# A decoder layer on one core: a fourth quad of w_down row tiles by Strassen's scheme with its first sum made by transfers, splits queued behind two merges, and a later load of x

## The chip, the cores and the metric

The kernel runs on one NeuronCore of a Trainium2 chip. A core has TensorE (matmuls, results into PSUM), VectorE, ScalarE and GpSimd (elementwise work), SyncE (here it only issues transfers), and 16 DMA engines that all queues share. Each engine works through its own queue in order and waits on semaphores of the others. The metric is device microseconds of one execution, given as the median of several runs; the profile is of one further execution.

## The reference

One layer on a sequence of 256 tokens of width 1024, all in float32:

```python
proj = x @ w_in                                   # three attention mixers read its columns
o_a, o_b, o_c = dsa_mixer(...), dilated_mixer(...), moba_mixer(...)
gates = sigmoid(x @ w_gate).reshape(256, 3, 1024)
merged = gates[:, 0] * (o_a @ w_br_a) + gates[:, 1] * (o_b @ w_br_b) + gates[:, 2] * (o_c @ w_br_c)
x = layer_norm(ALPHA * x + merged @ w_out, ln1_g, ln1_b)
h = square(relu(x @ w_up)) @ w_down               # 1024 -> 4096 -> 1024
ple = sigmoid(x @ w_ple_gate) * (p @ w_ple)
x = layer_norm(ALPHA * x + h + ple, ln2_g, ln2_b)
```

## The kernel before, in words

**Precision.** Every float32 operand is split in two float32r parts, `hi` (a copy in the shorter format, by ScalarE, line 75) and `lo` (the rest, a subtraction by VectorE, line 79), and a product is three matmuls, hi-hi, hi-lo and lo-hi (`prod`, line 134). Each weight is brought in as 128 x 1024 pieces of 512 KB and split as it arrives.

**`Weights` (lines 50 to 90)** keeps the list of these pieces in the order of their use. `get(i)` returns the split piece i and writes the instructions of all pieces up to i + `AHEAD` (4): a load on SP's queue into one of five `raw` buffers, the ScalarE cast, the VectorE subtraction into one of five `whi` and `wlo` buffers (or into a place given). `after` is a tuple of instructions: what is written while it is set is put behind them on their own engines' queues (`issue_after`), which fixes an order and adds no wait across engines. A scheduler then orders each queue from the written program, its priorities and its buffers.

**The stages.** After attention, `merge(p)` (line 559, four of them) multiplies the first branch into PSUM, forms the gated sum on VectorE (lines 568 and 569), and makes two row blocks `mt` by a scaling on ScalarE (line 572) and a subtraction on VectorE (line 573). `outp` (a `Wide`, line 524) is `merged @ w_out`: eight row tiles of `w_out`, four by `step` and four by `finish`, the last four split straight into a part of `hA` (shown as `hT`). `PL` first holds x: line 596 loads it, 1 MB, from ScalarE's queue, and line 597 the rows of the first layer norm (`rows1`, 1 MB broadcast). `ln1` (line 621) reads both. Then follow the `w_ple` product, `w_ple_gate`, and `w_up`: 32 blocks of 128 features (loop at line 676), whose squares are split into `hT` (plain) or, for the first 4 x `QUADS` blocks, gathered in `four`, summed (line 710) and split as a quad.

**`w_down` (lines 723 to 830).** Its 32 row tiles of 128 are contracted in two ways. A *plain* row tile takes 2 token blocks x 2 column halves x 3 matmuls of 512 columns. Four row tiles with the two token blocks and two column halves are a 2 x 2 by 2 x 2 block product, a *quad*: Strassen's scheme in Winograd's form needs 7 products instead of 8, each of 2 x 3 matmuls of 512 columns. Sums on the activation side are those of line 710; on the weight side `quad(u)` makes t1 = b - a, t2 = c - t1, t3 = c - b and t4 = d - t2 on VectorE (line 742) from the blocks a, b, c, d that SP loads (line 736). `order` mixes three quad products with two plain rows; the last `LAST` (6) plain rows are kept for the end, where each output block is finished in turn and normalised by `ln2` (line 815). Eight PSUM banks collect the products P1, P5, P6, P7 and the output blocks 11, 12, 21, 22; lines 803 to 813 add them. `rows2`, the second norm's rows, takes the buffer of `four` (tag `rows`, one buffer) and is loaded at line 724, ahead of the stage.

The change touches lines 40, 556 to 582, 596 and 597, 708 to 724, 735 to 757 and 802 to 811.

Of the kernel before, what the change touches and what calls it, by code (L numbers as in the profile page):

```python
# [11 lines left out]
F32 = mybir.dt.float32  # L12
F32R = mybir.dt.float32r
ALU = mybir.AluOpType
# [5 lines left out]
D = 1024  # L20
# [16 lines left out]
    0, 384, 448, 512, 1024, 1088, 1096, 1864, 2120, 2376, 2760, 3144)  # L37

AHEAD = 4
QUADS = 3  # L40
LAST = 6
FIRST = 4
DV = 640
# [50 lines left out]
def hybrid_layer(ctx: ExitStack, tc: tile.TileContext, x0, xn, pT, wqk, wva, wvb, wg, wbc, wba,  # L94
                 wout, wup, wdq, wdn, wpg, wple, lnrow, rel, mask, out):
    nc = tc.nc
    pe, act, dve, pool = nc.tensor, nc.scalar, nc.vector, nc.gpsimd

    keep = ctx.enter_context(tc.tile_pool(name="keep", bufs=1))
    raw = ctx.enter_context(tc.tile_pool(name="raw", bufs=5))  # L100
# [349 lines left out]
    for j in range(2):  # L450
# [8 lines left out]
        o = opair()  # L459
# [93 lines left out]
                    done(b, c, self.acc[b][c])  # L553

    T2 = (slice(0, 128), slice(128, 256))
    mt = []


    def merge(p):
        hi, lo = W.get(u_ba[p][0])  # L560
        ps = mmbank(512).rearrange("p (f s) -> p f s", f=2)
        for f in range(2):
            for k in range(3):
                c = slice((3 * f + k) * 128, (3 * f + k + 1) * 128)
                prod(ps[:, f], (hi[:, c], lo[:, c]), (op[:, k, 0], op[:, k, 1]), k == 0, k == 2)
        g6 = G[:, 6 * p:6 * p + 6].rearrange("p (f i) s -> p f i s", f=2)
        g = g6[:, :, 0]
        dve.scalar_tensor_tensor(g, g, 1.0, ps, op0=ALU.add, op1=ALU.mult)
        dve.tensor_tensor(g, g, g6[:, :, 1], op=ALU.add)
        for f in range(2):  # L570
            m = qpool.tile([128, 2, S], F32R, name="q", tag="q")
            act.mul(m[:, 0], g[:, f], 0.5)
            dve.scalar_tensor_tensor(m[:, 1], g[:, f], 0.5, m[:, 0].bitcast(F32), op0=ALU.mult,
                                     op1=ALU.subtract)
            mt.append(m)

    outp = Wide(u_out, lambda k, b: (mt[k][:, 0, T2[b]], mt[k][:, 1, T2[b]]))
    for p in range(4):
        merge(p)
    for k in range(4):  # L580
        outp.step(k)
    mid.close()


# [7 lines left out]
    def row_load(t, i):  # L592
        act.dma_start(t, lnrow[i:i + 2].rearrange("r d -> (r d)").partition_broadcast(128)
                      .rearrange("p (r d) -> p r d", r=2))

    act.dma_start(PL, xn)
    row_load(rows1, 0)

    st = {}

# [75 lines left out]
    for f in range(32):  # L676
        ps = mmbank(512).rearrange("p (b a t) -> p b a t", b=2, a=2)
        hi, lo = W.get(u_up[f][0])
        cs = [slice(k * 128, (k + 1) * 128) for k in range(KT)]
        for k in range(KT):  # L680
            pe.matmul(ps, lhsT=hi[:, cs[k]], rhs=x1[:, :, k], start=k == 0, stop=False)  # L681
        for k in range(KT):
            pe.matmul(ps[:, :, 0], lhsT=lo[:, cs[k]], rhs=x1[:, :, k, 0], start=False,  # L683
                      stop=k == KT - 1)
        r = w2.tile([128, 2, 128], F32, name="r", tag="r")
        dve.tensor_reduce(r, ps.rearrange("p b a t -> p b t a"), axis=AX.X, op=ALU.add)  # L686
        act.activation(r, r, AF.Relu)
        u, m = divmod(f, 4)
        if u >= QUADS:
            q = w2.tile([128, S], F32, name="q2", tag="q2")  # L690
            act.activation(q, r.rearrange("p b t -> p (b t)"), AF.Square)
            h = hT[:, f - 4 * QUADS]
            act.copy(h[:, 0], q)
            dve.tensor_tensor(h[:, 1], q, h[:, 0].bitcast(F32), op=ALU.subtract)
            continue
        g = four[:, u % 2]
        act.activation(g[:, :, m], r, AF.Square)
        if m % 2 == 0:
            continue
        hi, lo, y = ((hQ[:, u, 0, 0], hQ[:, u, 0, 1], g[:, 0, 0:2]) if m == 1 else  # L700
                     (hQ[:, u, 1:3, 0], hQ[:, u, 1:3, 1], g[:, :, 2:4]))
        act.copy(hi, y)
        dve.tensor_tensor(lo, y, hi.bitcast(F32), op=ALU.subtract)
        if m == 1:
            continue
        a11, a21, a12, a22 = g[:, 0, 0:2], g[:, 1, 0:2], g[:, 0, 2:4], g[:, 1, 2:4]
        z = w2.tile([128, 4, 2, 128], F32, name="s", tag="s", bufs=1)
        for o, a, b, f2 in ((0, a21, a22, ALU.add), (2, a11, a21, ALU.subtract),
                            (1, z[:, 0], a11, ALU.subtract), (3, a12, z[:, 1], ALU.subtract)):
            dve.tensor_tensor(z[:, o], a, b, op=f2)  # L710
        if u < 2:
            parts = [(z, hS[:, u, 0], hS[:, u, 1])]
            sums.append([(hS[:, u, 0, i], hS[:, u, 1, i]) for i in range(4)])
        else:
            ts = [[qpool.tile([128, 2, S], F32R, name="q", tag="q")
                   .rearrange("p m (j t) -> p m j t", j=2) for _ in range(2)] for _ in range(2)]
            parts = [(z[:, 2 * i:2 * i + 2], *ts[i]) for i in range(2)]
            sums.append([(ts[i // 2][0][:, i % 2], ts[i // 2][1][:, i % 2]) for i in range(4)])
        for y, hi, lo in parts:
            act.copy(hi, y)  # L720
            dve.tensor_tensor(lo, y, hi.bitcast(F32), op=ALU.subtract)

    rows2 = p3.tile([128, 2, D], F32, name="rows", tag="rows")
    row_load(rows2, 2)


    xw = x1.rearrange("p b k a s -> p (b k a s)").rearrange("p (k a c) -> p k a c", k=2, a=2)

    def quad(u):

        t = {}

        def load(*names):
            for n in names:
                t[n] = raw.tile([128, 1024], F32, name="raw", tag="raw")
                nc.sync.dma_start(t[n], wdq[u, "abcd".index(n)])
            return t[names[0]]

        def less(n, x, y):
            p = p3 if n == "t1" else raw  # L740
            t[n] = p.tile([128, 1024], F32, name="raw", tag="raw")
            dve.tensor_tensor(t[n], t[x], t[y], op=ALU.subtract)  # L742
            return t[n]

        A = [(hQ[:, u, m, 0], hQ[:, u, m, 1]) for m in range(3)]
        Z = sums[u]
        return [(lambda: load("a", "b"), A[0], "P1"), (lambda: less("t1", "b", "a"), Z[0], "P5"),
                (lambda: load("c"), Z[3], "12"), (lambda: less("t3", "c", "b"), Z[2], "P7"),
                (lambda: less("t2", "c", "t1"), Z[1], "P6"), (lambda: load("d"), A[1], "11"),
                (lambda: less("t4", "d", "t2"), A[2], "21")]  # L750

    todo = [x for u in range(QUADS) for x in quad(u)]
    plain = list(range(NP))
    order = []
    while todo:
        order += todo[:3] + plain[:2]
        todo, plain = todo[3:], plain[2:]
    order += plain
    left = {"P1": 2 * QUADS, "P5": 2 * QUADS, "P6": 2 * QUADS, "P7": 2 * QUADS,
            "11": 2 * QUADS + NP, "12": 2 * QUADS + NP, "21": 2 * QUADS + NP, "22": NP - LAST}  # L760
# [38 lines left out]
    p1, p5, p6, p7 = (acc["P" + n] for n in "1567")  # L799
    u2, u3 = Y[:, 0, H[0]], Y[:, 0, H[1]]  # L800
    blk = [[PL[:, b, H[c]] for c in range(2)] for b in range(2)]
    tt = lambda o, a, b: dve.tensor_tensor(o, a, b, op=ALU.add)
    tt(blk[0][0], p1, blk[0][0])
    act.copy(u3, p1)
    tt(u2, p6, u3)
    tt(u3, p7, u2)
    tt(u2, p5, u2)
    tt(blk[0][1], u2, blk[0][1])
    tt(blk[1][0], u3, blk[1][0])
    tt(u3, p5, u3)  # L810
    tt(blk[1][1], u3, blk[1][1])
    end = [[acc["11"], acc["12"]], [acc["21"]] + [next(ps_a)[:, 0:256] for _ in range(2)]]
    tt(blk[1][1], acc["22"], blk[1][1])
# [116 lines left out]
```

## Time and profile before

| | us |
|---|---|
| median of 3 runs | 442.63 (442.06 to 443.55) |
| the profiled execution | 442.14 |
| its span | 440.4 |
| from the first merge's stretch to TensorE's start on `w_out` | 193.0 to 206.3 |
| `w_up` stage | 259.6 to 348.95 |
| `w_down` stage, to TensorE's last matmul | 348.95 to 432.2 |

Each group's row of the profile names the line, the engine, the operation, what is written and read, and the mean time of one instruction. The waits say which engine was idle ahead of which line and what ended the idle time. The chain of waits is followed back from the last instruction: at each step to what released it, or to the instruction before it on its engine. A matmul of 512 columns shows 0.39 us of its own, but the next starts 0.23 us later, since they are pipelined; the time from start to start is what counts.

### The profile page before, as it was taken

The page shows a single profiled execution, that of the slowest core. Times are in us where ns is not written, and L with a number is a line of the kernel's source. Part 1 is how long each engine was busy: PE and PEld are TensorE (multiplying, and loading weights), DVE is VectorE, ACT ScalarE, POOL GpSimd, SP SyncE. Part 2 cuts the span into 40 slices and gives each one's busy share as a digit, 9 for nine tenths or more (in the row PEclk, how much of TensorE's full clock was granted, in tenths as well). Part 3 has the DMA queues.
Part 4 walks back from the last instruction along what each step waited for, and adds up shares of the span by engine and source line. Part 5 has one row for each costly group of instructions (what it writes and reads, how often), then busy time and mean ns, then how long its engine had stood idle before and what let it go on. Part 6 is the DMA issues. An engine that isn't in the chain of part 4 may idle for free.

```text
span 440.4 us, 7719 instructions
## 1 busy us (share of the span) xinstructions
PE 429.0 (97%) x2837; PEld 388.7 (88%) x2837; DVE 337.4 (77%) x602; ACT 269.8 (61%) x487; POOL 101.7 (23%) x98
## 2 busy tenths in 40 slices
PE   8999999999999999998999999999999999999992
PEld 8999999999999999998886888888888888888882
DVE  4978977475664588768958779999888978588956
ACT  6775375584787766855605567888877765456500
POOL 3564355397543644400001000000000000000001
PEclk9999999999999999999999999999999999999998
DMA  8896765448544345467860866668655364655502
GB/s 282 316 313 219 238 187 176 158 129 314 161 148 130 124 152 164 140 193 288 258 265 0 281 221 185 187 193 284 198 183 183 105 212 144 250 151 204 226 0 96
DMA packets 27113, 84.29 MB, mean 191 GB/s; under 512 B 2820, under 2 KB 6828, under 8 KB 26692
## 3 DMA queue, kind: packets, MB, share of 16 engines
q1 hardware_dynamic: 25872, 79.54, 55.5%
q10 hardware_dynamic: 1140, 4.19, 2.6%
q8 instruction: 22, 0.36, 0.3%
q14 instruction: 15, 0.12, 0.1%
q0 software_dynamic: 64, 0.07, 0.1%
HBM read 81.90 MB, written 1.90 MB: 190 GB/s over the span
## 4 chain that ended last, share of the span: by engine, by line
PE 93%; DVE 2%; DMA 2%; issue 2%; ACT 1%; POOL 0%; POOLq 0%; DVEq 0%; ACTq 0%
PE mm L134 39%; PE b L134 23%; PE mm L681 13%; PE mm L683 7%; PE b L273 3%; PE b L407 3%; DMA raw<-in_wout_dram 2%; PE b L129 1%; PE b L319 1%; ACT whi L75 0%; PE b L320 0%; PE b L322 0%; PE b L321 0%; PE b L312 0%; PE b L314 0%
## 5 line engine op out<-in xcount | busy, mean ns | idle before, releaser
L79 DVE TENSOR_TENSOR wlo<-raw,whi 128x1024 fp32r<-128x1024 f32 (+5 forms) x147 | 157.4, 1085 | 42.1 <-ACT whi L75 38.6
L75 ACT CAST whi<-raw 128x1024 fp32r<-128x1024 f32 (+3 forms) x147 | 147.8, 1011 | 57.4 <-PE mm L134 17.2
L79 POOL TENSOR_TENSOR wlo<-raw,whi 128x384 fp32r<-128x384 f32 (+3 forms) x58 | 77.3, 1342 | 81.8 <-ACT whi L75 67.2
L134 PE MATMUL mm<-xl,whi 128*128 128x256 f32 x336 | 95.5, 284 | 0.0
L134 PE MATMUL mm<-xh,whi 128*128 128x256 f32 x336 | 95.1, 283 | 0.0
L134 PE MATMUL mm<-xh,wlo 128*128 128x256 f32 x336 | 95.0, 283 | 0.0
L134 PEld LDWEIGHTS mm<-xl,whi 128*128 128x128 f32 x336 | 63.3, 188 | 0.9
L681 PE MATMUL mm<-x,whi 128*128 128x512 f32 x256 | 64.1, 392 | 0.0
L134 PEld LDWEIGHTS mm<-xh,wlo 128*128 128x128 f32 x336 | 63.3, 188 | 0.6
L134 PEld LDWEIGHTS mm<-xh,whi 128*128 128x128 f32 x336 | 63.3, 188 | 0.2
L612 POOL TENSOR_TENSOR rs<-rs,half 128x1 f32<-128x1 f32 x4 | 4.1, 1028 | 246.0 <-DVE rs L611 246.0
L134 PE MATMUL b<-whi,hT 128*128 128x512 f32 (+1 forms) x176 | 55.0, 379 | 0.0
L681 PEld LDWEIGHTS mm<-x,whi 128*128 128x128 f32 x256 | 46.1, 189 | 8.3
L134 PEld LDWEIGHTS b<-whi,hT 128*128 128x128 f32 x176 | 32.7, 188 | 6.2
L683 PEld LDWEIGHTS mm<-x,wlo 128*128 128x128 f32 x256 | 34.9, 190 | 2.5
L683 PE MATMUL mm<-x,wlo 128*128 128x256 f32 x256 | 35.7, 282 | 0.0
L134 PE MATMUL b<-wlo,hT 128*128 128x512 f32 (+1 forms) x88 | 33.4, 380 | 0.0
L686 DVE TENSOR_REDUCE r<-mm 128x256 f32<-128x512 f32 x32 | 22.0, 687 | 5.9 <-PE mm L683 5.9
L134 PE MATMUL mm<-op,whi 128*128 128x256 f32 x128 | 23.3, 281 | 0.0
L742 DVE TENSOR_TENSOR raw<-raw 128x1024 f32<-128x1024 f32 x12 | 14.7, 1222 | 9.2 <-DMA raw<-in_wdq_dram 9.2
L134 PE MATMUL b<-whi,x 128*128 128x512 f32 x64 | 20.5, 396 | 0.3 <-ACT x L634 0.3
L240 ACT ACTIVATE G<-mm 128x256 f32<-128x256 f32 x24 | 9.2, 382 | 18.3 <-PE mm L134 18.2
(171 smaller groups left out, 712.2 us busy)
## 6 DMA issues: line engine op xcount, KB each, us to landing
raw<-in_wup_dram SPq DMA_DIRECT2D x32, 512.0 KB
raw<-in_wg_dram SPq DMA_DIRECT2D x24, 512.0 KB
raw<-in_wdn_dram SPq DMA_DIRECT2D x20, 512.0 KB
raw<-in_wqk_dram SPq DMA_DIRECT2D x18, 512.0 KB
raw<-in_wdq_dram SPq DMA_DIRECT2D x12, 512.0 KB
raw<-in_wout_dram SPq DMA_DIRECT2D x8, 512.0 KB
raw<-in_wpg_dram SPq DMA_DIRECT2D x8, 512.0 KB
T<-tabd SPq DMA_DIRECT2D x24, 128.0 KB
```

The source lines that it names most:

```text
L75: nc.scalar.copy(hi, r)
L79: e.tensor_tensor(lo[:, c], r[:, c], hi[:, c].bitcast(F32), op=ALU.subtract)
L129: pe.transpose(t[:, 0:128], ident, ident)
L134: pe.matmul(ps, lhsT=a[x], rhs=b[y], start=first and i == 0, stop=last and i == 2)
L240: act.activation(G[:, n_g[0]], ps, AF.Tanh, scale=0.5)
L273: m = pe.matmul(ss[h][:, QC[b]], lhsT=q[d, x, c], rhs=k[d, y, 0:128 * (b + 1)], start=i == 0, stop=i == 2)
L319: pe.matmul(v[:, 0:S], lhsT=V[:, 0, vh], rhs=hi[:, 256:512], start=True, stop=False)
L407: pe.matmul(first[f], lhsT=w[:, k, 128 * f:128 * f + 128], rhs=x[:, k], start=k == i == 0, stop=k == KT - 1 and i == 2)
L681: pe.matmul(ps, lhsT=hi[:, cs[k]], rhs=x1[:, :, k], start=k == 0, stop=False)
L683: pe.matmul(ps[:, :, 0], lhsT=lo[:, cs[k]], rhs=x1[:, :, k, 0], start=False, stop=k == KT - 1)
L686: dve.tensor_reduce(r, ps.rearrange("p b a t -> p b t a"), axis=AX.X, op=ALU.add)
L742: dve.tensor_tensor(t[n], t[x], t[y], op=ALU.subtract)
```

## The change

`QUADS` goes from 3 to 4, so sixteen row tiles of `w_down` are done in quads and sixteen plainly, and `order` takes one plain row for each three quad products. The quad's first sum t1 is now a + b: SP loads b into one half of `pair`, and a transfer that GpSimd issues adds a onto it; the signs of the other sums and of P5 change with it. `pair` takes the buffer of `four`; the first two quads' t1 are asked for behind the `w_up` stage, the third's and fourth's when t2 of the first and second is made. t2 = t1 + c goes into a buffer of its own, t3 = t2 - a into a's, t4 = t2 + d into d's, and P6 now comes ahead of P7. `rows2` is loaded behind the stage's splits. After each of the first two merges `W.after` is set to that merge's last scaling and subtraction, so that splits written later queue behind these on ScalarE and VectorE, until the fourth `step` of `outp` is written. The loads of x and of `rows1` queue on ScalarE behind the scalings of the third merge.

```diff
-QUADS = 3
+QUADS = 4
...
-    mt = []
+    mt, muls = [], []
...
         for f in range(2):
             m = qpool.tile([128, 2, S], F32R, name="q", tag="q")
-            act.mul(m[:, 0], g[:, f], 0.5)
-            dve.scalar_tensor_tensor(m[:, 1], g[:, f], 0.5, m[:, 0].bitcast(F32), op0=ALU.mult,
-                                     op1=ALU.subtract)
+            muls.append(act.mul(m[:, 0], g[:, f], 0.5).ins)
+            low = dve.scalar_tensor_tensor(m[:, 1], g[:, f], 0.5, m[:, 0].bitcast(F32),
+                                           op0=ALU.mult, op1=ALU.subtract)
             mt.append(m)
+        if p < 2:
+            W.after = (muls[-1], low.ins)
...
     for k in range(4):
         outp.step(k)
+    W.after = ()
     mid.close()
...
-    act.dma_start(PL, xn)
-    row_load(rows1, 0)
+    with tc.issue_after(muls[5]):
+        act.dma_start(PL, xn)
+        row_load(rows1, 0)
...
-        for o, a, b, f2 in ((0, a21, a22, ALU.add), (2, a11, a21, ALU.subtract),
-                            (1, z[:, 0], a11, ALU.subtract), (3, a12, z[:, 1], ALU.subtract)):
+        for o, a, b, f2 in ((0, a21, a22, ALU.subtract), (2, a11, a21, ALU.subtract),
+                            (1, z[:, 0], a11, ALU.subtract), (3, a12, z[:, 1], ALU.add)):
...
-    rows2 = p3.tile([128, 2, D], F32, name="rows", tag="rows")
-    row_load(rows2, 2)
-
+    pair = p3.tile([128, 2, D], F32, name="rows", tag="rows")
+
+    def first_sum(u):
+
+        if u < QUADS:
+            nc.sync.dma_start(pair[:, u % 2], wdq[u, 1])
+            pool.dma_start(pair[:, u % 2], wdq[u, 0], accum_op=ALU.add)
+
+    for u in range(2):
+        first_sum(u)
...
-        def load(*names):
-            for n in names:
-                t[n] = raw.tile([128, 1024], F32, name="raw", tag="raw")
-                nc.sync.dma_start(t[n], wdq[u, "abcd".index(n)])
-            return t[names[0]]
-
-        def less(n, x, y):
-            p = p3 if n == "t1" else raw
-            t[n] = p.tile([128, 1024], F32, name="raw", tag="raw")
-            dve.tensor_tensor(t[n], t[x], t[y], op=ALU.subtract)
+        def load(n):
+            t[n] = raw.tile([128, 1024], F32, name="raw", tag="raw")
+            nc.sync.dma_start(t[n], wdq[u, "abcd".index(n)])
+            return t[n]
+
+        def have():
+            t["t1"] = pair[:, u % 2]
+            return t["t1"]
+
+        def make(n, x, y, f):
+            t[n] = t[y]
+            if n == "t2":
+                t[n] = p3.tile([128, 1024], F32, name="raw", tag="raw")
+            dve.tensor_tensor(t[n], t[x], t[y], op=f)
+            if n == "t2":
+                first_sum(u + 2)
             return t[n]
...
-        return [(lambda: load("a", "b"), A[0], "P1"), (lambda: less("t1", "b", "a"), Z[0], "P5"),
-                (lambda: load("c"), Z[3], "12"), (lambda: less("t3", "c", "b"), Z[2], "P7"),
-                (lambda: less("t2", "c", "t1"), Z[1], "P6"), (lambda: load("d"), A[1], "11"),
-                (lambda: less("t4", "d", "t2"), A[2], "21")]
+        return [(lambda: load("a"), A[0], "P1"), (have, Z[0], "P5"),
+                (lambda: load("c"), Z[3], "12"),
+                (lambda: make("t2", "t1", "c", ALU.add), Z[1], "P6"),
+                (lambda: make("t3", "t2", "a", ALU.subtract), Z[2], "P7"),
+                (lambda: load("d"), A[1], "11"),
+                (lambda: make("t4", "t2", "d", ALU.add), A[2], "21")]
...
-        order += todo[:3] + plain[:2]
-        todo, plain = todo[3:], plain[2:]
+        order += todo[:3] + plain[:1]
+        todo, plain = todo[3:], plain[1:]
...
-    tt = lambda o, a, b: dve.tensor_tensor(o, a, b, op=ALU.add)
+    rows2 = p3.tile([128, 2, D], F32, name="rows", tag="rows")
+    row_load(rows2, 2)
+    tt = lambda o, a, b, f=ALU.add: dve.tensor_tensor(o, a, b, op=f)
...
-    tt(u2, p5, u2)
+    tt(u2, p5, u2, ALU.subtract)
...
-    tt(u3, p5, u3)
+    tt(u3, p5, u3, ALU.subtract)
```

## The prediction

> **What bounds the kernel now.** I read the page's busy shares, its 40 slices and its chain first, then the waits of TensorE, then stretches of the program.
>
> ```profile
> PE 429.0 (97%) x2837; PEld 388.7 (88%) x2837; DVE 337.4 (77%) x602; ACT 269.8 (61%) x487; POOL 101.7 (23%) x98
> ...
> PEclk9999999999999999999999999999999999999998
> ...
> PE 93%; DVE 2%; DMA 2%; issue 2%; ACT 1%; POOL 0%; POOLq 0%; DVEq 0%; ACTq 0%
> ```
>
> TensorE is busy 97% of the span at the full granted clock, and 93% of the chain that ended last is its work. So a change pays in two ways only: fewer matmuls, or less time in which TensorE waits. The waits of TensorE, then four stretches (length, PE, PEld, DVE, ACT, POOL, clock, DMA share, GB/s):
>
> ```profile
> PE b L129 <- POOL ident masks.py:199: 1.6, 1, 1.6
> PE b L134 <- ACT q L572: 1.1, 1, 1.1
> PE b L134 <- ACT x L634: 0.3, 1, 0.3
> ...
> 193.00:206.27 13.27, 12.16 (x106) 11.96 (x104) 9.98 (x15) 7.02 (x11) 0.00 (x0) 1.00 0.79 277
> 206.27:235.00 28.73, 28.71 (x128) 23.22 (x128) 23.93 (x37) 12.54 (x20) 1.01 (x1) 1.00 0.64 220
> 259.60:348.95 89.35, 89.35 (x513) 78.65 (x513) 81.22 (x114) 70.60 (x125) 0.00 (x0) 1.00 0.61 189
> 348.95:428.00 79.05, 79.05 (x351) 65.44 (x351) 63.20 (x63) 39.92 (x43) 0.00 (x0) 1.00 0.51 173
> ```
>
> The change touches two waits' worth of ground: the 1.1 us ahead of the first `w_out` matmul, and the `w_down` stage (from 348.95), in which TensorE never waits at all. There only the number of matmuls counts, as long as VectorE, ScalarE and the transfers keep the split weights coming.
>
> **Part 1: splits behind the merges, x later.** TensorE, ScalarE and VectorE around the gap, and SP's loads:
>
> ```profile
> 204.88 0.28 PE L134 MATMUL mm<-op,wlo 128*128 128x256 f32 x1
> 206.27 0.50 PE L134 MATMUL b<-whi,q 128*128 128x512 f32 x1 [1.11 <-ACT q L572]
> ...
> 196.74 0.34 ACTq L596 DMA_DIRECT2D PL<-in_xn_dram  x1
> 203.90 1.05 ACT L75 CAST hT<-raw 128x1024 fp32r<-128x1024 f32 x1 [3.21 <-DMA raw<-in_wout_dram]
> 204.86 1.04 ACT L75 CAST whi<-raw 128x1024 fp32r<-128x1024 f32 x1
> 205.80 0.72 ACT L572 ACTIVATE q<-G 128x256 fp32r<-128x256 f32 x2
> ...
> 199.73 0.68 DVE L568 SCALAR_TENSOR_TENSOR G<-G,mm 128x512 f32<-128x512 f32 x1
> 200.72 1.23 DVE L79 TENSOR_TENSOR wlo<-raw,whi 128x1024 fp32r<-128x1024 f32 x1 [0.31 <-ACT whi L75]
> 201.86 0.69 DVE L569 TENSOR_TENSOR G<-G 128x512 f32<-128x512 f32 x1
> 204.99 1.23 DVE L79 TENSOR_TENSOR hT<-raw,hT 128x1024 fp32r<-128x1024 f32 x1 [1.84 <-ACT hT L75]
> ...
> 197.10 6.72 DMA raw<-in_wout_dram
> ...
> 186.18 20.39 SPq L71 DMA_DIRECT2D raw<-in_wout_dram  x8
> 226.60 0.69 DVE L622 SCALAR_TENSOR_TENSOR Y<-PL,b 128x512 f32<-128x512 f32 x1 [4.48 <-PE b L134]
> ```
>
> TensorE ends the merges at 204.88 + 0.28 = 205.16. Merge 0's sum is there at 202.55, but its scaling (`q`, 205.80) stands in ScalarE's queue behind two splits, the first of which waited 3.21 us for a `w_out` load that took 6.72 us; the 1 MB of x, issued at 196.74, travelled beside it. With the hold, L568 ends at 200.41, L569 follows without the split between (+0.69 = 201.1), two scalings of 0.36 end near 201.8: 3.4 us before TensorE is free. The split of `w_out` 1 then takes 1.05 + 1.23 and ends near 204.1; its matmuls come 12 x 0.2267 = 2.72 us after 205.16, at 207.9. Splits 2 and 3 wait for merge 1, some 2 us later, and end near 206.2 and 207.4; due at 210.6 and 213.3. The held splits queue nothing else but their own followers on ScalarE and VectorE, and VectorE's idle 1.84 us fills with merge work. So the gap goes: **-1.11 us**.
>
> x (`PL`) now starts behind merge 2's scalings, about 206, and takes the first layer-norm row load with it. Its first reader is L622 at 226.60, some 20 us on, and 2 MB at the 371 GB/s quoted below is 5.7 us. But it moves onto `w_out` 7, whose load is issued as SP's last of eight, at the latest 206.57. If that now takes the 6.72 us, it lands at 213.3 and is split at 215.6; TensorE starts the last four row tiles at 205.16 + 48 x 0.2267 = 216.0. Cover of 0.4 us, plus the two microseconds in which tiles 4 to 6 go first. I cost it at nothing; without that cover it costs what exceeds it (rival 1).
>
> **Part 2: a fourth quad.** A stretch of the chain, VectorE's pieces, and the stage's groups:
>
> ```profile
> 387.05 6.12 PE b L134 x27
> ...
> 370.58 4.62 DVE L79 TENSOR_TENSOR wlo<-raw,whi 128x1024 fp32r<-128x1024 f32 x4
> ...
> L742 DVE TENSOR_TENSOR raw<-raw 128x1024 f32<-128x1024 f32 x9 | 11.0, 1223 | 8.3 <-DMA raw<-in_wdq_dram 8.3
> L75 ACT CAST whi<-raw 128x1024 fp32r<-128x1024 f32 x35 | 36.8, 1054 | 24.4 <-PE mm L134 15.3 <-DVE raw L742 3.1 <-PE b L134 2.1
> ...
> 409.00:414.00 5.00, 5.00 (x24) 4.14 (x23) 4.86 (x7) 2.88 (x4) 0.00 (x0) 1.00 0.95 371
> ```
>
> A matmul 512 wide takes 6.12 / 27 = 0.2267 us. Four row tiles cost 4 x 12 = 48 of them plainly, 7 products x 6 = 42 in a quad. One quad more saves six: **-1.36 us** (366 to 360 in the stage). Nothing in TensorE's other work changes.
>
> The feed has to bear it. One product lasts 1.36 us, a plain row 2.72. Per quad the new order (three products, one row) holds 7 products and 2.33 rows, 15.87 us of TensorE. VectorE then has 9.33 splits and 3 sums, 12.33 pieces of 4.62 / 4 = 1.155, or 14.2 us: 90%. The old order gave 15.67 pieces (four sums) in 22.2 us: 81%, and the row shows 63.20 of 79.05. ScalarE has 9.33 casts of 1.05, 9.8 us. The transfers: five per quad and 2.33 rows of 0.524 MB, 3.84 MB in 15.87 us, 242 GB/s, against 371 seen. VectorE's waits above were for quad loads (8.3 us), with five raw buffers of which old quads took seven per turn; the new ones take three, since t3 and t4 are made in place. So the feed has less to wait for and less room; I cost it at nothing, for ScalarE's casts wait mostly for TensorE to free a part buffer (15.3 of 24.4 us).
>
> In the `w_up` stage the fourth quad adds four small sums and three splits to VectorE in place of four small splits:
>
> ```profile
> L710 DVE TENSOR_TENSOR s<-rows,s x3: 412/416/417, 278.4 to 300.7; 128x256 f32<-128x256 f32 x3
> ...
> 281.94:293.11 11.17, 11.17 (x65) 9.83 (x64) 10.57 (x17) 8.95 (x16) 0.00 (x0) 1.00 0.67 191
> 304.28:315.45 11.17, 11.17 (x65) 9.83 (x65) 9.35 (x15) 9.62 (x20) 0.00 (x0) 1.00 0.75 264
> ```
>
> 4 x 0.42 + 0.42 + 0.68 (half a 1.23 piece and start-up) + 1.23 - 4 x 0.42 = 2.3 us. A whole quad fills 10.57 of 11.17 us of VectorE, so a fourth one fits, and behind it 1.8 us are idle. Nothing.
>
> **The first sum by transfers.** It frees VectorE of four pieces (counted above) and adds, per quad, one SP load into `pair` and one adding transfer that GpSimd issues. They need the buffer of `four`, whose last reader ran at 300.7; a quad later that is 312. The first quad's old sum was made here, and GpSimd's only transfers of this kind are these:
>
> ```profile
> 332.10 1.23 DVE L742 TENSOR_TENSOR raw<-raw 128x1024 f32<-128x1024 f32 x1 [0.85 <-DMA raw<-in_wdq_dram]
> ...
> tab<-in_rel_dram POOLq DMA_DIRECT2D x1, 36.0 KB, 5.9
> ```
>
> So load and add have 20 us for the first quad, and for the third and fourth the 12 products and 4 rows between t2 of one quad and P5 of the next but one, 12 x 1.36 + 4 x 2.72 = 27.2 us. No row shows an adding transfer. Lower bound: 0.524 MB at 371 GB/s, 1.4 us. Upper: the 36 KB took 5.9 us in 24 rows; by rows, 128 would take 31 us. I take 5.9 + 1.4 = 7.3 us, the small transfer being the nearest row and mostly fixed; with a load of at most 6.72 us before it that is 14 us, hidden. SP, in order, holds its later loads behind the `pair` load while that waits for t2; but t2 is also what frees c's raw buffer for them. GpSimd has nothing behind it until the last norm.
>
> The Trainium skill's page "DMA: Bandwidth & Descriptors" (Anatomy of one DMA) gives a transfer issued by GpSimd about 2.0 us plus bytes / 436e3; by that estimate the add takes 3.2 us, and the sum stays as it is.
>
> The second norm's rows, 1 MB loaded at about 301 before, now wait for the last t2, near 395, and are read at about 426. The last six weights come in that stretch, near the limit of 371 GB/s; 1 MB more is 2.8 us of it.
>
> ```profile
> 417.94 1.22 DVE L79 TENSOR_TENSOR x<-raw,x 128x1024 fp32r<-128x1024 f32 x1
> ...
> 422.83 1.53 PE L134 MATMUL b<-x,hT 128*128 128x512 f32 x6
> 428.70 1.41 DVE L617 SCALAR_TENSOR_TENSOR Y<-Y,mv,rows 128x512 f32<-128x512 f32 x2
> ```
>
> The last split ends at 419.16, its matmuls start at 422.83: 3.7 us of cover, so nothing. The tail's sums are as many as before.
>
> **Sum.** The profiled execution took 442.14 us (span 440.4 and 1.74 around it). 442.14 - 1.11 - 1.36 = 439.67. The median shown is 0.49 higher, so **440.2** in its terms.
>
> **Rivals.**
> 1. *The wait moves.* x and the row load meet `w_out` 7 and `w_ple`; TensorE waits there for what it gained. For: the cover is 0.4 us, and one load beside x took 6.72. Against: tiles 4 to 6 go first. 442.63 - 1.36 = 441.3.
> 2. *VectorE becomes the bound in `w_down`* (nothing left of the gain). t2, t3 and t4 hang on each other and each goes through a cast before its split; if VectorE idles a cast's 1.05 us at each, a quad costs 14.2 + 3.15 = 17.4 us against 15.87, +1.5, four quads +5.9. It decides from 0.56 us of idle per sum. Four tiles split ahead (5.4 us) cover a part; I take half: 440.2 + 3.2 = 443.4. Against: the old order idled on loads, and its raw buffers were scarcer.
> 3. *The adding transfers land late* (slower). At the upper 31 us plus 6.72, P5 of the third quad waits 38 - 27 = 11 us, and that of the first some 3: about 454. It decides from 20 us. The skill's page "SBUF — State Buffer" (SBUF: two separate sides) says that GpSimd cannot write descriptors while VectorE runs in a two-port mode, which would speak for this; its section "Who interferes with whom" excepts `tensor_tensor`, the kind that L79 and L742 are, and no run here shows either.
>
> **Chances.** About 0.3% (1.33 us) is what a measurement of this kernel can tell from no change: faster is below 441.3, slower above 444.0. Forecast 0.60 (0.03 of it above 441.3), rival 1 0.22 (half on each side), rival 2 0.12 (two thirds within 0.3%), rival 3 0.06. Faster 0.57 + 0.11 = 0.68, same 0.03 + 0.11 + 0.08 = 0.22, slower 0.04 + 0.06 = 0.10. Range: 439.0 (the 0.3 us wait at L634 gone too, and the runs' spread) to 443.3, which leaves out half of rival 2, rival 3 and some 0.06 below.
>
> **What would show it.** Part 1 is right if TensorE's wait for `q` is gone and no wait for `wout`, `wple` or PL takes its place between 205 and 235; part 2 if the stage from the last `w_up` matmul to TensorE's end is 1.4 us shorter with no wait in it, and VectorE busy near 90%. Waits of P5's cast for `pair` would show rival 3, waits of TensorE for L79 rival 2. A changed order of the program before 190 us would make all of it wrong.

## The result, and the profile after

The changed kernel takes 439.26 us (median of 9 runs, 438.07 to 441.34) against 442.38 (9 runs) beside it; the ratio is 0.9929, 95% interval 0.9907 to 0.995. Beside later runs it took 440.07 us (7 runs), ratio 0.9938 (0.9915 to 0.996). The profiled execution took 438.31 us, its span 436.5 against 440.4. Two executions, one of 708.56 us of the kernel before (granted clock 0.56) and one of 528.18 us of the held tail below (0.75), are left out of all ratios and spreads here. The forecast of 440.2 lies 0.9 us above the first of these medians and 0.1 above the second, inside the spread of the runs. Its parts do not agree so well, as will be seen.

The page of the changed kernel, its busy shares and its chain:

```profile
PE 425.7 (98%) x2831; PEld 387.8 (89%) x2831; DVE 342.2 (78%) x609; ACT 272.5 (62%) x490; POOL 105.5 (24%) x102
...
PE 97%; issue 1%; POOL 0%; DVE 0%; POOLq 0%; DVEq 0%
```

All waits of TensorE in it (engine, line, for what; us in total, times, longest):

```profile
PE b L129 <- POOL ident masks.py:199: 1.6, 1, 1.6
```

TensorE has 2831 matmuls and transposes in place of 2837, is 97% of the chain, and after its first microseconds waits for nothing that the profile shows: the waits for `q` (1.1 us) and for L634 (0.3 us) are gone. That does not say where 3.8 us of span (440.36 - 436.52) went. For this the program is cut at the first matmul of each stage. The columns run from TensorE's first matmul on the mixers' outputs (`op`; these begin among the attention's matmuls and end as the merges) to the first of `w_out`; from there to the first of `w_up`; and from the first of `w_down` to the end of the span. `w_up` took 89.36 us in every kernel of this study. The time ahead of the first column lay between 143.96 and 146.11; the changed kernel alone had 144.66 in one profile and 146.11 in the other.

| kernel (one profile each) | `op` to `w_out` | `w_out` to `w_up` | `w_down` to end | median us of the runs beside it | ratio to before (95%) |
|---|---|---|---|---|---|
| before | 61.52 | 53.15 | 91.58 | | |
| changed | 60.32 | 50.92 | 91.26 | 439.26 | 0.9929 (0.9907 to 0.995) |
| changed, again | 60.24 | 51.71 | 91.23 | 440.07 | 0.9938 (0.9915 to 0.996) |
| part 1 alone | 60.25 | 50.86 | 91.55 | 439.3 | 0.9919 (0.99 to 0.9938) |
| part 1 alone, again | 60.24 | 51.57 | 91.57 | 439.73 | 0.994 (0.9921 to 0.996) |
| hold alone | 60.24 | 51.39 | 91.57 | 439.49 | 0.9918 (0.9896 to 0.994) |
| later x alone | 60.28 | 53.94 | 91.56 | 441.55 | 0.9971 (0.9956 to 0.9986) |
| part 2 alone | 61.69 | 53.13 | 91.25 | 443.26 | 1.0012 (0.9993 to 1.0032) |
| changed, `w_ple` early | 60.24 | 57.55 | 92.78 | 444.43 | 1.0054 (1.0028 to 1.0081) |
| changed, first sums on VectorE | 60.24 | 51.58 | 91.39 | 439.26 | 0.9917 (0.9901 to 0.9933) |
| changed, tail held | 60.25 | 50.86 | 90.59 | 438.09 | 0.9898 (0.9879 to 0.9916) |
| changed, tail held, again | 60.24 | 51.29 | 90.61 | 439.74 | 0.9936 (0.9909 to 0.9963) |
| part 1, tail held | 60.25 | 50.86 | 91.41 | 438.78 | 0.9917 (0.9896 to 0.9937) |
| changed, sums on VectorE, tail held | 60.28 | 51.00 | 91.07 | 437.88 | 0.9895 (0.9877 to 0.9913) |

So the change brought 61.52 - 60.32 = 1.20 us in the merges, 53.15 - 50.92 = 2.23 us between `w_out` and `w_up` (1.44 by its second profile), and 91.58 - 91.26 = 0.32 us in `w_down` and the end. The forecast had 1.11, nothing, and 1.36. In the merges' own stretch the gain is the gap alone: from the last merge matmul to the first of `w_out` it was 206.27 - 204.88 = 1.39 us before and is 0.12 in the changed kernel.

**The 2.23 us.** The stretch from `w_out` to `w_up` as the windows give it (length, PE, PEld, DVE, ACT, POOL, clock, DMA share, GB/s), first of the kernel before, then of the changed one:

```profile
206.27:259.42 53.15, 52.75 (x232) 41.96 (x233) 41.38 (x57) 24.94 (x34) 2.00 (x2) 1.00 0.60 206
```

```profile
204.98:255.90 50.92, 50.92 (x235) 42.19 (x233) 40.52 (x54) 24.87 (x32) 2.01 (x2) 1.00 0.70 247
```

The same matmuls, at the same clock. In the kernel before TensorE counts as busy for 52.75 of 53.15 us, and yet 2.23 us could be taken out. The busy share hides it: a matmul's row lasts 0.39 us where the next can start 0.2267 us on, so a start that comes up to 0.16 us late leaves no gap between the rows. The weight loads, which are not stretched in that way, show it: 41.96 of 53.15 is 79%, 42.19 of 50.92 is 83%. (The Trainium skill's page "Perfetto Trace Analysis", Identifying the Most-Contended Engine, says that matmul busy time is no good measure of how near TensorE is to its limit and that the share of the weight loads is one to use; these two rows agree.) The place is seen in the timeline of the kernel before, around the transposes of the first layer norm (start, length, engine, line; the releaser in brackets):

```profile
233.72 0.39 PE L134 MATMUL mm<-whi,pl 128*128 128x512 f32 x1
233.95 1.03 PE L632 MATMUL b<-ident,Y 128*128 128x128 f32 x8
235.28 0.50 PE L134 MATMUL b<-whi,x 128*128 128x512 f32 x1 [0.29 <-ACT x L634]
235.62 0.40 PE L134 MATMUL b<-wlo,x 128*128 128x512 f32 x1
236.00 0.73 PE L134 MATMUL b<-whi,x 128*128 128x512 f32 x2
...
238.65 1.32 PE L632 MATMUL b<-ident,Y 128*128 128x128 f32 x8
239.98 0.50 PE L134 MATMUL b<-whi,x 128*128 128x512 f32 x1
240.32 0.40 PE L134 MATMUL b<-wlo,x 128*128 128x512 f32 x1
```

Eight transposes run in one piece, and the matmuls behind them start 0.34 and 0.38 us apart where 0.2267 is the shortest distance, since each needs what ScalarE and VectorE have just made of the transposes. Against 0.1 us for a transpose (below, eight take 0.84) and 0.2267 for a matmul, each group with the four matmuls behind it loses 0.9 us, and the matmul ahead of the second 0.24; with 0.36 us of late starts behind the wait for `q` that is 2.4 us. The changed kernel at the same place, with ScalarE and VectorE ahead of it:

```profile
215.35 1.05 ACT L75 CAST hT<-raw 128x1024 fp32r<-128x1024 f32 x1 [5.84 <-DMA raw<-in_wout_dram]
...
216.44 1.23 DVE L79 TENSOR_TENSOR hT<-raw,hT 128x1024 fp32r<-128x1024 f32 x1 [2.71 <-ACT hT L75]
...
222.79 0.68 DVE L626 SCALAR_TENSOR_TENSOR Y<-PL,b 128x512 f32<-128x512 f32 x1
...
230.89 0.60 PE L636 MATMUL b<-ident,Y 128*128 128x128 f32 x4
231.24 0.48 PE L134 MATMUL mm<-whi,ph 128*128 128x512 f32 x1
...
232.72 0.60 PE L636 MATMUL b<-ident,Y 128*128 128x128 f32 x4
233.08 0.48 PE L134 MATMUL b<-whi,x 128*128 128x512 f32 x1
...
233.62 1.03 PE L636 MATMUL b<-ident,Y 128*128 128x128 f32 x8
234.46 0.73 PE L134 MATMUL b<-whi,x 128*128 128x512 f32 x2
```

The first eight transposes come as four and four with six `w_ple` matmuls between them, the next eight follow at 233.62 with their input ready, and no start is late by more than 0.12 us, 0.3 in all. What changed is the order of TensorE. In the kernel before, 12 of the 24 `w_ple` matmuls ran between those of `w_out`; they put off the first layer norm by 12 x 0.2267 = 2.7 us, and left 12 matmuls to cover it. Now all 24 come behind `w_out`. The layer norm's first step starts 222.79 - 204.98 = 17.81 us behind the first `w_out` matmul, where it was 226.60 - 206.27 = 20.33, and twice as much work covers its chain.

### The profile page after: what moved, and what is told of

Same layout as the page of the kernel before. It is cut to its first block, busy times and chain, and to the rows that moved or that the text cites. A ratio compares the mean times of both kernels' runs of the same rounds, so it can differ in the third digit from the quotient of the medians.

```text
span 436.5 us, 7727 instructions
## 1 busy us (share of the span) xinstructions
PE 425.7 (98%) x2831; PEld 387.8 (89%) x2831; DVE 342.2 (78%) x609; ACT 272.5 (62%) x490; POOL 105.5 (24%) x102
## 4 chain that ended last, share of the span: by engine, by line
PE 97%; issue 1%; POOL 0%; DVE 0%; POOLq 0%; DVEq 0%
PE mm L134 42%; PE b L134 24%; PE mm L685 13%; PE mm L687 7%; PE b L273 3%; PE b L407 3%; PE b L129 1%; PE b L319 1%; PE b L322 0%; PE b L320 0%; PE b L321 0%; PE b L312 0%; PE b L314 0%; PE b L636 0%; PE b L313 0%
## 5 line engine op out<-in xcount | busy, mean ns | idle before, releaser
L79 DVE TENSOR_TENSOR wlo<-raw,whi 128x1024 fp32r<-128x1024 f32 (+5 forms) x146 | 156.2, 1086 | 42.8 <-ACT whi L75 39.5
L75 ACT CAST whi<-raw 128x1024 fp32r<-128x1024 f32 (+3 forms) x146 | 146.2, 1011 | 51.6 <-PE b L134 15.6
L79 POOL TENSOR_TENSOR wlo<-raw,whi 128x384 fp32r<-128x384 f32 (+3 forms) x58 | 77.5, 1345 | 81.5 <-ACT whi L75 70.7
L134 PE MATMUL b<-whi,hT 128*128 128x512 f32 (+1 forms) x164 | 51.0, 379 | 0.0
L134 PEld LDWEIGHTS b<-whi,hT 128*128 128x128 f32 x164 | 30.6, 188 | 5.8
L733 POOL DMA_DIRECT2D rows<-in_wdq_dram x4 | 3.5, 884 | 127.6 <-PE mm L685 81.8
L134 PE MATMUL b<-wlo,hT 128*128 128x512 f32 (+1 forms) x82 | 30.9, 379 | 0.0
```

Source lines behind the costliest of these rows:

```text
L75: nc.scalar.copy(hi, r)
L79: e.tensor_tensor(lo[:, c], r[:, c], hi[:, c].bitcast(F32), op=ALU.subtract)
L134: pe.matmul(ps, lhsT=a[x], rhs=b[y], start=first and i == 0, stop=last and i == 2)
```

## The experiments

The theory (A): the hold reorders TensorE, and `w_ple`'s matmuls as filler (work that TensorE can do while it would wait) around the first layer norm give the 2.23 us. The rivals: x's later transfer gives it, by leaving the transfers of the merges alone (B), or it belongs to part 2 (C).

**Which part does it?** Four kernels undo or take alone a part each. *Part 1 alone* is the kernel before with the hold and the later x (the lines that keep the list `muls` are left out here and below):

```diff
+        if p < 2:
+            W.after = (muls[-1], low.ins)
...
-    act.dma_start(PL, xn)
-    row_load(rows1, 0)
+    with tc.issue_after(muls[5]):
+        act.dma_start(PL, xn)
+        row_load(rows1, 0)
```

> The kernel before with part 1 alone (the hold of the split queue, x and the first layer-norm rows later), three quads as before. Theory A (the hold changes the order of TensorE's matmuls: all 24 w_ple matmuls are left as filler around the first layer norm, and this is worth 2.2 us beyond the 1.1 us wait for q): the wait for q is gone, first w_out matmul to first w_up matmul takes 51.1 us as in the changed kernel (before: 53.3), and the stretch from the first w_down matmul to the last add stays as before; about 439.0 us, ratio 0.992. Theory B (the 2.2 us come from x's later transfer, which frees the transfers in the merges): the same here. Theory C (the 2.2 us belong to part 2): 53.3 us there and about 441.3 us, ratio 0.9975.

The stretch is 50.86 us, the wait for `q` is gone, the time 439.3 us and the ratio 0.9919: theory C falls. Its TensorE order around the transposes is that of the changed kernel (four, six `w_ple` matmuls, four). *Part 2 alone* is the changed kernel without these lines:

> The changed kernel without the hold and with x loaded where it was before: the fourth quad and the adding transfers alone. Theories A and B: the wait of 1.1 us for q is there, first w_out to first w_up matmul takes 53.3 us as before, and the w_down stage is 1.3 us shorter in its matmuls but only 0.4 to 0.7 us at the end of the program, since the last adds follow block (1,0) by 4.6 us of VectorE; about 441.9 us, ratio 0.9988. If the 1.36 us counted in full: 441.0, ratio 0.997. Theory C (the 2.2 us belong to this part): 51.1 us, and about 439.5 us.

```profile
PE b L134 <- ACT q L572: 1.3, 1, 1.3
PE b L134 <- ACT x L634: 0.3, 1, 0.3
```

Both waits of before are back in its list of TensorE's waits, and the stretch is 53.13. `w_down` to the end takes 91.25, 0.33 less than before, and in the runs not even that is left: 443.26 us where 441.9 was expected, 1.0012 (0.9993 to 1.0032). All that can be measured of the change is part 1. *The hold alone* leaves x where it was:

```diff
+        if p < 2:
+            W.after = (muls[-1], low.ins)
```

> The kernel before with the hold alone; x and the rows are loaded as early as before. Theory A: w_ple's 24 matmuls lie behind w_out's 96, the wait for q is gone or below 0.3 us, first w_out to first w_up matmul takes 51.1 to 51.6 us; about 439.2 us, ratio 0.993. Theory B (x's later transfer is what gives it): 53.3 us in that stretch and 441.3 us or more.

51.39 us and 0.9918: the hold does it, and theory B falls. The missing 0.5 us against part 1 alone is one late group left, in its timeline:

```profile
232.92 0.39 PE L134 MATMUL mm<-whi,pl 128*128 128x512 f32 x1
233.15 1.03 PE L635 MATMUL b<-ident,Y 128*128 128x128 f32 x8
234.48 0.50 PE L134 MATMUL b<-whi,x 128*128 128x512 f32 x1 [0.29 <-ACT x L637]
```

Here all 24 `w_ple` matmuls ran out ahead of the transposes and none stands between them. The runs do not show this half microsecond (439.49 us against 439.3). *The later x alone*:

```diff
-    act.dma_start(PL, xn)
-    row_load(rows1, 0)
+    with tc.issue_after(muls[5]):
+        act.dma_start(PL, xn)
+        row_load(rows1, 0)
```

> The kernel before with x and the first layer-norm rows loaded later, behind merge 2's scalings, and no hold. Theory A: the wait for q stays at 0.7 to 1.1 us (the queue of splits is the same; the load that the first split waited for may come earlier), the first w_ple matmuls still lie between w_out's, and first w_out to first w_up matmul takes 52.5 to 53.3 us; about 442.0 us, ratio 0.999. Theory B: 51.1 us there, and about 439.5 us.

The stretch is 53.94 us, longer than before and outside the 52.5 to 53.3 that was expected. The first `w_out` matmul no longer waits, but the ninth does, since the second block of the merge's sum still stands behind a split on ScalarE and VectorE:

```profile
205.88 0.40 PE L134 MATMUL b<-wlo,q 128*128 128x512 f32 x1
207.39 1.42 PE L134 MATMUL b<-whi,q 128*128 128x512 f32 x5 [1.12 <-DVE q L573]
```

Both columns together take 114.22 against 114.67 us: later x is worth 0.45 us by itself, without the hold. (Its runs say 0.9971, which is 1.3 us; its profile came to the first column 0.8 us earlier than that of before, in a stage that the edit does not touch. What the runs have beyond 0.45 us is open.)

**Is it the filler?** In *the changed kernel with `w_ple` early* 18 of the 24 matmuls stand ahead of `w_out`'s last four row tiles:

```diff
...
+    pss = [ple_mm(0, 0), ple_mm(0, 1), ple_mm(1, 0)]
+    with ExitStack() as held:
+        for _, i in pss:
+            held.enter_context(tc.issue_after(i))
+        for b in range(2):
+            for c in range(2):
+                for k in (4, 5, 6, 7):
+                    outp.go(k, b, c)
...
```

> The changed kernel with 18 of the 24 w_ple matmuls put ahead of w_out's last four row tiles, so that 6 are left around the first layer norm. Theory A, made narrower by the runs so far (a group of eight transposes that TensorE runs in one piece costs it 0.9 to 1.1 us in the matmuls behind it; filler between the transposes hides that): at least one group of eight runs in one piece again, first w_out to first w_up matmul takes 52.0 to 53.1 us (changed kernel 50.9), and the time rises by 1.0 to 2.2 us. Theory B (x's later transfer): 50.9 us, no change. Rival E (the transposes cost the same wherever filler stands, and the gain is that w_out's last tiles end sooner): no slow starts behind the transposes, and 52.5 us or more all the same.

The direction is right and the size wrong: 57.55 us, 6.6 more, where 1.0 to 2.2 was expected. Two groups of eight transposes run in one piece again, each with a late start behind it (0.52 and 0.47 us, and 0.1 to 0.3 in the matmuls that follow). The rest is an effect of my edit: the `w_ple` weights were not split yet when TensorE came to them. Its list of waits:

```profile
PE mm L134 <- ACT whi L75: 2.3, 1, 2.3
...
PE b L134 <- DVE wlo L79: 1.2, 1, 1.2
```

The 2.3 us and the slow matmuls behind it lie at 216 to 223 us, on `w_ple`. The slow ones start 0.43 us apart, and the windows show why: the granted clock (third number from the end) is 0.51 there, and 0.2267 / 0.51 is 0.44 us.

```profile
219.90:223.40 3.50, 3.50 (x9) 2.82 (x9) 3.34 (x3) 1.78 (x2) 0.00 (x0) 0.51 0.99 401
```

The time of this kernel as a whole therefore proves nothing, but its two losses lie apart in the trace and can be added up, as what each start has beyond 0.2267 us (0.105 for a transpose). Ahead of the first transpose that is 5.1 us, 0.1 in the changed kernel. From the first transpose to `w_up` it is 1.8 us, against 0.2 in the changed kernel and 2.0 in the kernel before. The hold and the later x are both in this kernel, and what its edit changes is the place of `w_ple`; so the order brings back 1.6 us at the transposes, inside what was expected. Rival E of the expectation, for which there would be no late starts there, falls. The order of the kernels above agrees: two late groups 53.15 and 53.13, one 51.39, none 50.86 and 50.92.

**How much cover is left?** The *changed kernel again*:

> The changed kernel once more, beside the next three on the same chip. About 439.2 us, ratio 0.993; its runs spread over some 3 us as before (438.07 to 441.34), where part 1 alone spread over 0.6 us.

The same program took 51.71 us in the stretch in place of 50.92. Its timeline, to be read against that of the changed kernel above:

```profile
217.49 1.06 ACT L75 CAST hT<-raw 128x1024 fp32r<-128x1024 f32 x1 [6.51 <-DMA raw<-in_wout_dram]
...
218.58 1.22 DVE L79 TENSOR_TENSOR hT<-raw,hT 128x1024 fp32r<-128x1024 f32 x1 [3.48 <-ACT hT L75]
...
224.94 0.68 DVE L626 SCALAR_TENSOR_TENSOR Y<-PL,b 128x512 f32<-128x512 f32 x1
...
234.76 0.40 PE L134 MATMUL b<-wlo,x 128*128 128x512 f32 x1
235.35 1.32 PE L636 MATMUL b<-ident,Y 128*128 128x128 f32 x8 [0.20 <-DVE Y L623]
```

Its first `w_out` matmul is at 206.35. Counted from there `w_out` 7, which is loaded beside x, was cast 217.49 - 206.35 = 11.14 us on, 10.37 in the first profile. From there the delay runs down VectorE's queue: its split starts 218.58 - 206.35 = 12.23 us behind the first `w_out` matmul (11.46 there), the layer norm's first step 18.59 (17.81), and the second group of transposes waits. The nine profiles with part 1's order give a curve. With that split at 10.4 to 11.5 us the stretch takes 50.86 to 51.00; at 11.82, 51.29; at 12.06 and 12.08, 51.57 and 51.58; at 12.23, 51.71. The cover ends near 11.5 us, and from there each further microsecond costs about one.

**What are the adding transfers worth?** The *changed kernel with the first sums on VectorE* keeps SP's load of b and adds a on VectorE:

```diff
             nc.sync.dma_start(pair[:, u % 2], wdq[u, 1])
-            pool.dma_start(pair[:, u % 2], wdq[u, 0], accum_op=ALU.add)
...
             t["t1"] = pair[:, u % 2]
+            dve.tensor_tensor(t["t1"], t["a"], t["t1"], op=ALU.add)
```

> The changed kernel with each quad's first sum made by VectorE in place instead of by the adding transfer: four pieces of 1.17 us more on VectorE in w_down. If VectorE has room (86% busy there in the changed kernel, 92% with these): no wait of TensorE for a split, w_down's matmuls take 81.2 us as in the changed kernel, same time within 0.3 us, so the adding transfers were not needed. If 90% is the limit: TensorE waits for L79 by 1 to 4 us. If the adding transfers are what spreads the runs of kernels with part 2, the runs of this one lie within 1.5 us of each other and its median is some 0.5 us below the changed kernel's; otherwise they spread over 3 us as well.

```profile
346.18:427.36 81.18, 81.18 (x375) 67.78 (x374) 72.90 (x75) 41.47 (x44) 0.88 (x1) 1.00 0.52 162
```

From the first `w_down` matmul to the start of their last group in the timeline its VectorE is busy 72.90 of 81.18 us, 90%, TensorE waits for nothing, and the matmuls take 81.18 us against 81.23 in the changed kernel. The time is 439.26 us, 0.9917. The adding transfers buy nothing that can be measured here: VectorE had the room.

They were not late either. The changed kernel's view of them, and what VectorE waited for at the `rows` tiles:

```profile
L733 POOL DMA_DIRECT2D rows<-in_wdq_dram x4: 849/870/946, 314.1 to 362.5; - x4
...
DMA to landing us min/median/max: 7.0/8.8/9.3
```

```profile
L757 DVE TENSOR_TENSOR raw<-rows,raw x4: 1224/1224/1226, 328.8 to 386.4; 128x1024 f32<-128x1024 f32 x4
...
  DMA raw<-in_wdq_dram: 5.2, 4
```

The transfers land in 7.0 to 9.3 us. What the sum t2 waits for is the load of c, 5.2 us in four waits. VectorE stands still in these, with splits queued behind. In the profiles of kernels with adding transfers such a wait lasts 0.90 to 3.25 us, and once, in the kernel with `w_ple` early, the longest was more than the splits made ahead could bear. TensorE and VectorE there:

```profile
379.94 1.23 DVE L772 TENSOR_TENSOR raw<-rows,raw 128x1024 f32<-128x1024 f32 x1 [3.25 <-DMA raw<-in_wdq_dram]
...
382.35 0.50 PE L134 MATMUL b<-wlo,hT 128*128 128x512 f32 x1 [1.25 <-DVE wlo L79]
```

With the sums on VectorE t2 no longer waits; t1 does, by 0.2 to 1.6 us. That fits the spread of the runs: in the six sets of kernels with adding transfers they lie 2.1 to 6.1 us apart, in the six with the hold and without them 0.6 to 1.8. But the kernel before, which has none, spread over 3.7 us beside the last four. Of the changed kernel and the held tail none of the slowest executions was profiled; the profiled one of the kernel with `w_ple` early, 446.47 us where its runs begin at 442.93, is the one with the wait above. That the transfers cause the spread is argued, not shown.

**Where is the fourth quad's gain?** In the changed kernel the matmuls, from the first to the start of the last group of `w_down`, take 81.23 us, 1.29 less than before (82.52), about what six matmuls should. The end of the program moved by 0.32. The last blocks' adds tell why. The kernel before, then the changed one:

```profile
428.03 0.69 DVE L817 TENSOR_TENSOR Y<-b,PL 128x512 f32<-128x512 f32 x1 [0.15 <-PE b L134]
...
432.61 0.41 DVE L817 TENSOR_TENSOR Y<-b,PL 128x256 f32<-128x256 f32 x1
```

```profile
413.46 0.51 PE L134 MATMUL b<-wlo,hT 128*128 128x256 f32 x2
...
417.91 0.28 PE L134 MATMUL b<-wlo,hT 128*128 128x256 f32 x1
418.03 0.28 PE L134 MATMUL b<-whi,hT 128*128 128x256 f32 x1
...
423.82 0.69 DVE L838 TENSOR_TENSOR Y<-b,PL 128x512 f32<-128x512 f32 x1
...
426.41 0.41 DVE L838 TENSOR_TENSOR Y<-b,PL 128x256 f32<-128x256 f32 x1
...
428.39 0.41 DVE L838 TENSOR_TENSOR Y<-b,PL 128x256 f32<-128x256 f32 x1
```

Of the 36 matmuls of 256 columns of the last two blocks, six run ahead of the last of block (1,0), whose add is at 423.82; in the kernel before it was one. It comes 78.56 us behind the first `w_down` matmul, 0.69 earlier than before (79.25), not 1.29. From that add VectorE is the bound: 428.39 - 423.82 = 4.57 us to the last one, 4.58 before. A *held tail* takes that back (`prod` returns its last matmul for it):

```diff
+            with ExitStack() as held:
+                if b == 1 and c > 0:
+                    held.enter_context(tc.issue_after(tail))
                 for i, (hi, lo) in enumerate(ws):
-                    prod(end[b][c], ...)
+                    tail = prod(end[b][c], ...)
```

> The changed kernel with the matmuls of the last two blocks, 256 wide, held behind those of block (1,0). If the missing part of the fourth quad's gain lies in the 14 or so of them that run ahead of block (1,0)'s end: first w_down matmul to block (1,0)'s add takes 76.9 to 77.9 us in place of 78.6, and the time falls by 0.6 to 1.5 us, to 437.7 to 438.6 us, as far as VectorE's last pieces follow. If the end is set by the last matmul (all are needed for it): w_down's matmuls still take 81.2 us, the last add comes no sooner, and the time stays.

```profile
422.54 0.69 DVE L839 TENSOR_TENSOR Y<-b,PL 128x512 f32<-128x512 f32 x1
...
425.25 0.42 DVE L839 TENSOR_TENSOR Y<-b,PL 128x256 f32<-128x256 f32 x1
...
427.24 0.41 DVE L839 TENSOR_TENSOR Y<-b,PL 128x256 f32<-128x256 f32 x1
```

Block (1,0)'s add now comes 422.54 - 344.79 = 77.75 us behind the first matmul, and `w_down` to the end takes 90.59 us, 0.67 less than in the changed kernel. None of the 256-wide matmuls runs ahead now; the six that did account for it (6 x 0.12 = 0.7 us), and not the 14 or so that I had expected. The runs gave 438.09 us, 0.9898.

The last four, on one chip, were to settle what the quad and the hold are worth. The base, the same hold with three quads, and the held tail once more:

> Part 1 alone once more, beside the next three on the same chip, as the base for what the fourth quad is worth. About 439.3 us, ratio 0.992, runs within 1 us of each other.

> Part 1 alone (three quads) with the last two blocks held behind block (1,0). In part 1 alone the matmuls of the last blocks follow block (1,0) nearly in order (its add to the last matmul: 3.28 us, 3.39 with the hold in the changed kernel, 2.67 without it). If the fourth quad loses its gain because its order lets some six of them run ahead, the hold brings this kernel 0 to 0.3 us, and the changed kernel with the hold stays 0.7 to 1.3 us ahead of this one. If the hold is worth the same 0.6 us here, the fourth quad is worth nothing either way.

> The changed kernel with the last two blocks held, once more beside part 1 alone: 438.1 us, ratio 0.990, 1.0 us below part 1 alone if the fourth quad's matmuls count once the tail is in order; 439 us, level with it, if the first measurement was luck.

By the profiles, the held tail brings part 1 alone 0.14 to 0.16 us (91.41 against 91.55 and 91.57), as expected, and with the tail in order the fourth quad is worth 91.41 - 90.61 = 0.80 us. The runs do not bear this out: 439.73, 438.78 and 439.74 us, with intervals that overlap, and the fourth quad not ahead. By the condition set in the last expectation above, the first 438.09 of the held tail was luck, in part at least; its runs now lie between 437.29 and 442.69. What the fourth quad is worth in device time stays open. The last kernel takes both edits, VectorE's sums and the held tail:

> The changed kernel with VectorE's first sums in place of the adding transfers and with the last two blocks held: a candidate better than both. First w_down matmul to the end 90.4 to 90.8 us (changed kernel 91.2, its hold alone 90.6), about 438.1 us, ratio 0.990. If the adding transfers, or the waits of the sums behind c's load, spread the runs, these lie within 1.2 us of each other and the median is some 0.3 us below the hold alone; if VectorE's extra 4.7 us now count, it is 0.5 us or more above.

437.88 us (437.31 to 438.28), 0.9895 (0.9877 to 0.9913): the lowest median of this study, with the least spread of the kernels with four quads, though its `w_down` to the end, 91.07, is 0.5 us longer than the held tail's in the profile and longer than was expected. The first add of the last blocks comes 0.9 us later there (75.9 us behind the first `w_down` matmul, 75.0 in the held tail), and VectorE goes on from it without a gap; why TensorE ends that block later is open. Its median stands 1.9 us below the held tail with adding transfers and 0.9 below part 1 with the held tail, all on the same chip, but the intervals of the three overlap.

## Why the prediction came out right

The time was right by luck: two errors cancel.

- **Part 1, the gap.** Forecast -1.11; measured 60.32 - 61.52 = -1.20 in the merges. The step is right: the hold brings `q` ahead of the splits, and in the first profile no wait for `wout`, `wple` or PL on TensorE takes its place.
- **Part 1, the rest of the stretch.** The forecast had nothing here. The sentence that failed is "Nothing in TensorE's other work changes." The wait list of before showed 0.3 us at L634, which I kept for the edge of the range; the loss there was 2.2 us, as late starts inside what counts as busy, and the hold reordered the `w_ple` matmuls so that they cover it. Part 1 is worth 3.43 us by the first profile of the changed kernel, 2.72 by the second, and 2.7 to 3.6 by the runs of part 1 alone: some three times its term.
- **Part 2, six matmuls.** Forecast -1.36, and the matmuls are 1.29 us shorter. But the sum took them in full to the end, where 0.32 arrived in the profile, and in the runs nothing that can be measured. It left out that the last six rows' order lets 256-wide matmuls run ahead (0.6 us given back), with VectorE as the bound behind, and some 0.4 us at the very end, which the last section names.
- **VectorE near 90%.** 67.17 of 78.56 us, 86%, and no wait of TensorE for L79: rival 2 did not come. The room is larger than I feared, for 90%, in the kernel with the sums on VectorE, did no harm either.
- **Adding transfers.** I took 7.3 us; they landed in 7.0 to 9.3, inside the bounds and hidden by the windows of 20 and 27.2: rival 3 fell. By the estimate from the Trainium skill's page "DMA: Bandwidth & Descriptors" (Anatomy of one DMA) they would have taken 3.2 us; the measurement decides, and it is more than twice that.
- **Rival 1, the wait moves onto `w_out` 7.** The wait did come, 4.9 to 6.5 us on ScalarE in the kernels with part 1, but at the row tile itself the matmuls of tiles 4 to 6 covered it. Where it costs is 7 us on, in the layer norm behind it on VectorE: 0 to 0.8 us, from execution to execution. I had looked for it at the wrong reader. Of the two loads only x moved: ScalarE issues it at 206.22 us, as forecast, in place of 196.74, but the rows of the first norm at 218.01, where it was 219.41.

## What to carry over

A busy engine can still be late: compare starts with the shortest distance between them, or the share of the weight loads, before a stage is called full. A hold on one queue can be worth most through the order that it gives to another; look where filler goes, and whether work without a deadline (here `w_ple`) stands behind the chain that it can cover. A matmul saved counts at the end only if the last result comes sooner by as much, so order the tail by what the last block needs.

## What was unexpected

- The row of the last two stores on SP is 0.86 us long in every profile without adding transfers and 1.06 to 1.08 us in every one with them (eight profiles and six). Each issue in it takes 0.33 us in all of them, so it is the second that starts later, 0.73 to 0.75 us behind the first in place of 0.53. Why is open. This is of the kernel before, and of the changed one:

```profile
436.08 0.86 SPq L823 DMA_DIRECT2D out_dram<-Y  x2
```

```profile
431.87 1.06 SPq L844 DMA_DIRECT2D out_dram<-Y  x2
```

- From the start of VectorE's last two pieces (L619 in the kernel before, L623 in the changed one) to the end of the span it is 5.17 to 5.19 us in all profiles with three quads and 5.50 to 5.59 in all with four, with adding transfers or without. What the 0.3 to 0.4 us are is open; no kernel was made for it.
- The split of `w_out` 7 starts 10.41 and 12.06 us behind the first `w_out` matmul in two executions of part 1 alone, one program, and the stretch behind it differs by 0.7 us: two profiles of the same kernel are not the same to better than that.
